# An HGRN and MLA kernel on one core: rotated keys computed a head earlier, work moved between the engines, the last norm by halves

## The chip, the cores and the metric

The kernel runs on one core of a Trainium2 chip. The metric is the device time of one execution in microseconds (us), given as the median of several runs. A core has engines that run side by side, each in the order of its own queue: TensorE (PE in the profile; PEld is its weight load), VectorE (DVE), ScalarE (ACT), GpSimd (POOL), and SyncE (SP), which here only issues DMAs. Matmuls leave their sums in PSUM, and DVE or ACT evacuate them to SBUF.

## The reference, cut to what matters

Two blocks follow one another. The first (SSD mixer with sliding-window attention, then a convolutional FFN) works on 512 tokens and 16 meta tokens. The second, where most of the change lies, is:

```
u  = rms_norm(h)                       # 512 tokens x 1024
hq, hf, hi, hz, cq, ckv, kr, mz, g = split(u @ w_in2)
y1 = hgrn2(hq, hf, hi, hz)             # 8 heads of 128, chunks of 32 tokens
q  = rms_norm(cq)  @ w_uq              # 8 heads of 128 + 64 rotated
k, v = split(rms_norm(ckv) @ w_ukv)    # 8 heads of 128 and 128
k_pe = rope(kr)                        # 64 wide, shared by all heads
y2 = softmax(mask(q_nope k_nope^T + rope(q_pe) k_pe^T)) v * silu(mz)
h  = h + (sigmoid(g1) * (y1 @ wa) + sigmoid(g2) * (y2 @ wb)) @ w_out2
out = rms_norm(h)
```

`rope` takes halves x1, x2 to x1 cos - x2 sin and x2 cos + x1 sin. All is fp32.

## The kernel before, in words

Tokens lie along the free axis and features on the 128 partitions. An fp32 product is made of three products in a faster format (fp32r): activations and weights are each split into a high part and a rest, and `gemm` (L80) issues, per slot of 128 input features, high x high (L88), high weights x rest of the activations (L89) and rest of the weights x high activations (L90). `wload` (L66) brings 512 KB of weights by an SP DMA into one of two `wraw` buffers; ACT copies the high part (`whi`, L76) and DVE subtracts it (`wlo`, L77), or POOL where `eng=nc.gpsimd` is given, as for MLA's `w_uk` and `w_uq` (in `mla_a`, L1111 and L1117). `whi` and `wlo` have three buffers each. PSUM is given out by tags: `g` (2 buffers, for gemms), `a` (3, scores), `t` (2, transposes and sums), `o` (1).

The start (`load`) brings the hidden state, splits it (DVE, `ul`, L62), sums squares on ACT, POOL and DVE, and broadcasts the reciprocal norms R (L129 on PE, L131 on ACT). Projections of the unnormed state start before R is there; R is multiplied in when a result is evacuated (`mulR`, L845).

The second block runs by `Block2.run` (L1203). For each HGRN head h, `hgrn_a(h+1)` projects and prepares the next head and `hgrn_b(h)` runs the chunks; between them stand pieces for MLA (`lora_jobs`): two parts of the latent keys and three of the latent queries with their sums of squares, then at h = 7 their norms and `kpe`. `kpe` (L1043) projects the shared rotated keys, 24 matmuls of 512 columns from a weight tile whose 128 columns hold the 64 features twice, evacuates them times R, rotates them (`rope`, L1077: four DMAs that swap quarters of the partitions, t x sin on DVE L1081, x x cos on POOL L1082, the sum on DVE L1083), and splits them into `kph` (ACT, L1051) and `kpl` (DVE, L1055). `mla_v` (L1085) then makes V, eight groups of six matmuls, each evacuated by ACT with the norm as its scale (`vt`, L1103). For each head, `mla_a` projects keys and queries (and rotates the queries of two heads at a time), `mla_split` splits them (L59 on DVE, `kl` and `ql`), `mla_b` makes scores (L1161 to L1166), the maximum on DVE (L1167), the exponent on ACT, and transposes (L1178), and `mla_c` multiplies by V (L1197).

`output` (L1229) merges the branches with gates. The product with `w_out2` has eight tiles of 128 features: six over all 512 tokens, the last two by halves of 256 tokens. `add` (L1269) adds each to the residual; `SumSq` squares on ACT (L151), adds on POOL (L159) and sums over partitions on PE (L169); `rsqrt` is eleven small DVE steps (L107 to L112). `finish` broadcasts the result over the partitions (PE, L1285), copies it to SBUF (`Rf`, ACT, L1287), multiplies residual, gain and R (six of eight tiles in one DVE step, L1295; the other two on ACT, L1292, and POOL, L1293) and sends each tile of 128 KB out (L1296).

The order on each engine is not that of the code alone: a scheduler places the instructions, moving blocks under `high_priority` forward, and tiles' buffers tie the engines together. In the first block it fills attention's waits on PE with rows of other gemms: `ps_t` L645 are transposes of the probabilities, `pt` L646 and L650 their evacuations on ACT, L655 and L656 the products with the values, `q` L657 the evacuation of a pair of heads, and `gate` L673 a gate between them.

## Time and profile before

| what | value |
|---|---|
| median of three runs | 1815.54 us (1814.12 to 1816.58) |
| profiled execution | 1814.76 us |
| its span, first to last instruction | 1813.0 us |
| mean granted TensorE clock | 0.991 |
| PE busy | 1760.3 us, 12068 matmul records |
| DVE, ACT, POOL busy | 1133.0, 751.5, 319.1 us |

A profile page gives one execution; its views are the busy time of each engine, tables of stretches of time with the clock that TensorE was granted, groups of instructions by line, timelines of an engine, and the chain of waits that ended last. A row such as `1432.79 2.85 DVE lf L1083` says when a step started, how long it took, and where; square brackets at a timeline's row give the idle time before it and what ended it.

### The profile page before, as it was taken

To read this page: it belongs to the slowest core of one execution; us is meant where nothing else is said; L and a number is where in the kernel's file an instruction comes from. 1 tells how busy PE (TensorE), PEld (TensorE's weight loads), DVE (VectorE), ACT (ScalarE), POOL (GpSimd) and SP (SyncE) were. 2 spreads that over 40 slices of the span, in tenths; PEclk is the share of its full clock that TensorE was granted. 3 is DMA by queue.
4 is the path that set the end of the run, shared out by engine and by line. 5 is a ranking of instruction groups with operands and counts; after the bars stand their busy time and mean duration, and the time that the engine had idled before them with its cause. 6 is when DMAs were issued, how large, how long until landed. Compare 5 with 4: busy or idle time off the path is not lost.

```text
span 1813.0 us, 29822 instructions
## 1 busy us (share of the span) xinstructions
PE 1760.3 (97%) x12068; PEld 1588.7 (88%) x12068; DVE 1133.0 (62%) x2140; ACT 751.5 (41%) x1326; POOL 319.1 (18%) x300
## 2 busy tenths in 40 slices
PE   7999999999999999999999999999999999999997
PEld 7989999999989889999999888878888777788886
DVE  7797777855587645466666533576665467743543
ACT  4544444432346643344444433554342445632232
POOL 2154444533320002200000011100000121000112
PEclk9999999999999999999999999999999999999999
DMA  4323232222222122222222222222112121222222
GB/s 146 102 87 104 82 106 83 95 94 94 88 84 76 63 94 94 94 82 94 94 94 94 87 96 96 82 93 70 70 70 93 56 72 48 71 93 93 93 93 71
DMA packets 51311, 158.34 MB, mean 87 GB/s; under 512 B 5923, under 2 KB 9765, under 8 KB 51173
## 3 DMA queue, kind: packets, MB, share of 16 engines
q1 hardware_dynamic: 49252, 153.91, 24.7%
q10 hardware_dynamic: 1872, 2.39, 0.4%
q8 instruction: 95, 1.56, 0.3%
q14 instruction: 44, 0.35, 0.1%
q0 software_dynamic: 48, 0.13, 0.0%
HBM read 152.93 MB, written 2.16 MB: 86 GB/s over the span
## 4 chain that ended last, share of the span: by engine, by line
PE 85%; DVE 7%; ACT 3%; issue 2%; POOL 1%; DMA 1%; SPq 0%; DVEq 0%; POOLq 0%; ACTq 0%
PE ps_g L88 22%; PE ps_g L89 22%; PE ps_g L90 22%; PE ps_g L813 2%; PE ps_g L814 2%; PE ps_g L812 2%; DVE wlo L77 1%; DMA E<-csd 1%; DVE cv L339 1%; PE ps_o L1197 1%; POOL xe L393 1%; PE ps_t L645 1%; PE ps_a L956 1%; PE ps_a L443 1%; PE ps_t L412 1%
## 5 line engine op out<-in xcount | busy, mean ns | idle before, releaser
L76 ACT ACTIVATE whi<-wraw 128x1024 fp32r<-128x1024 f32 (+2 forms) x265 | 274.9, 1038 | 585.9 <-PE ps_g L89 369.8
L77 DVE TENSOR_TENSOR wlo<-wraw,whi 128x1024 fp32r<-128x1024 f32 (+3 forms) x259 | 333.7, 1289 | 152.7 <-ACT whi L76 151.6
L88 PE MATMUL ps_g<-uh,whi 128*128 128x256 f32 (+2 forms) x1056 | 305.5, 289 | 2.4 <-DVE z L186 1.4
L90 PE MATMUL ps_g<-uh,wlo 128*128 128x256 f32 (+2 forms) x1056 | 301.9, 286 | 0.0
L89 PE MATMUL ps_g<-ul,whi 128*128 128x256 f32 (+2 forms) x1056 | 301.2, 285 | 0.0
L88 PEld LDWEIGHTS ps_g<-uh,whi 128*128 128x128 f32 x1056 | 200.2, 190 | 4.8 <-DVE z L186 1.6
L89 PEld LDWEIGHTS ps_g<-ul,whi 128*128 128x128 f32 x1056 | 200.0, 189 | 0.4 <-issue 0.2
L90 PEld LDWEIGHTS ps_g<-uh,wlo 128*128 128x128 f32 x1056 | 199.8, 189 | 0.4 <-issue 0.3
L88 PE MATMUL ps_g<-fh,whi 128*128 128x256 f32 (+1 forms) x704 | 199.1, 283 | 0.8 <-DVE fx L186 0.8
L89 PE MATMUL ps_g<-fl,whi 128*128 128x258 f32 (+1 forms) x704 | 199.5, 284 | 0.0
L90 PE MATMUL ps_g<-fh,wlo 128*128 128x258 f32 (+1 forms) x704 | 198.3, 282 | 0.0
L88 PE MATMUL ps_g<-vh,whi 128*128 128x512 f32 x464 | 185.0, 399 | 1.8 <-DVE lf L845 1.8
L90 PE MATMUL ps_g<-vh,wlo 128*128 128x512 f32 x464 | 184.5, 398 | 0.3 <-DVE wlo L77 0.3
L89 PE MATMUL ps_g<-vl,whi 128*128 128x512 f32 x464 | 184.4, 397 | 0.0
L159 POOL TENSOR_TENSOR sq<-sq 128x514 f32<-128x514 f32 (+2 forms) x48 | 61.9, 1299 | 495.7 <-ACT sq L151 495.7
L88 PEld LDWEIGHTS ps_g<-fh,whi 128*128 128x128 f32 x704 | 133.7, 190 | 1.0 <-DVE fx L186 1.0
L89 PEld LDWEIGHTS ps_g<-fl,whi 128*128 128x128 f32 x704 | 134.0, 190 | 0.0
L90 PEld LDWEIGHTS ps_g<-fh,wlo 128*128 128x128 f32 x704 | 133.6, 190 | 0.0
L88 PEld LDWEIGHTS ps_g<-vh,whi 128*128 128x128 f32 x464 | 87.3, 188 | 20.3 <-ACT whi L76 2.2
L90 PEld LDWEIGHTS ps_g<-vh,wlo 128*128 128x128 f32 x464 | 87.3, 188 | 19.0 <-DVE wlo L77 0.8
L89 PEld LDWEIGHTS ps_g<-vl,whi 128*128 128x128 f32 x464 | 87.4, 188 | 18.9
L88 PE MATMUL ps_g<-yh,whi 128*128 128x256 f32 (+1 forms) x256 | 75.3, 294 | 1.5 <-DVE bt L480 1.1
(434 smaller groups left out, 3834.9 us busy)
## 6 DMA issues: line engine op xcount, KB each, us to landing
wraw<-in_w_in SPq DMA_DIRECT2D x128, 512.0 KB, 3.3
wraw<-in_w_ffn_in SPq DMA_DIRECT2D x44, 512.0 KB, 3.1
E<-csd SPq DMA_DIRECT2D x32, 265.0 KB, 3.9
wraw<-in_w_ssd SPq DMA_DIRECT2D x16, 512.0 KB, 3.2
wraw<-in_w_out SPq DMA_DIRECT2D x16, 512.0 KB, 3.2
wraw<-in_w_ffn_out SPq DMA_DIRECT2D x16, 512.0 KB, 3.2
wraw<-in_w_pab SPq DMA_DIRECT2D x16, 512.0 KB, 3.3
wraw<-in_w_att SPq DMA_DIRECT2D x8, 512.0 KB, 3.3
```

Of the source, the lines that this page charges most:

```text
L76: nc.scalar.activation(hf[:, :n], raw[:, :n], AF.Copy)
L77: (eng or nc.vector).tensor_tensor(lf[:, :n], raw[:, :n], hf[:, :n].bitcast(F32), ALU.subtract)
L88: nc.tensor.matmul(ps, wh, a, start=(i == 0), stop=False)
L89: nc.tensor.matmul(ps, wh, b, start=False, stop=False)
L90: nc.tensor.matmul(ps, wl, a, start=False, stop=(i == last))
L159: self.g.nc.gpsimd.tensor_tensor(a[:, :self.ntok], a[:, :self.ntok], sq[:, :self.ntok], ALU.add)
L339: nc.vector.scalar_tensor_tensor(cv, xr[:, j:j + NT], w(j), cv, ALU.mult, ALU.add)
L393: nc.gpsimd.tensor_tensor(xe[:CH].rearrange("p c (h d) -> p c h d", h=2), xd[:CH, 0:4, :].rearrange("p c (h d) -> p c h d", h=2), dtx(0, 4 ...
L412: nc.tensor.matmul(px[:, c * 128:(c + 1) * 128], bt[:CH, c, :], xe[:CH, c, :], start=True, stop=True)
L812: nc.tensor.matmul(ps, wh, uh, start=(k == 0), stop=False)
L813: nc.tensor.matmul(ps, wh, ul, start=False, stop=False)
L814: nc.tensor.matmul(ps, wl, uh, start=False, stop=(k == NFF - 1))
```

## The change

1. `load`: the broadcast of R is put under high priority.
2. At the start, twelve matmuls of a tile of ones with itself, which nothing uses, are put ahead of the others.
3. `kpe`: the high part and the rest of the 64 weight columns lie side by side in one tile of 128, so that one matmul makes both products with the high activations, and a second one, 64 columns wide, the product with their rest: 16 matmuls instead of 24. Both halves of the partitions are rotated, two further DMAs swap the halves, and DVE adds them. `kpe` is called at h = 6 in place of h = 7.
4. `rope`: x x cos goes from POOL to DVE.
5. `mla_v`: every second group of V is evacuated by DVE.
6. The weights of `mla_a` are split by DVE.
7. `block_input` is called for other heads at a time.
8. `output`: three tiles by halves; the gains are multiplied in on ACT beforehand, so that `finish` has one multiply by R for two tiles of a half (three on DVE, one on POOL) and sends 256 KB at a time.

```diff
-            bcast_rows(g, self.R, rsqrt(g, ps[:88, :6], 88, 6, 1.0 / D, "h"), 88, 6, NT)
+            with g.tc.high_priority():
+                bcast_rows(g, self.R, rsqrt(g, ps[:88, :6], 88, 6, 1.0 / D, "h"), 88, 6, NT)
...
-            self.mulR(k, self.win(base + 2), self.R)
+            with g.tc.high_priority():
+                raw = g.wp.tile([128, 8, 128], F32, name="wraw", tag="wraw", bufs=2)
+                nc.sync.dma_start(out=raw.rearrange("p a b -> p (a b)"), in_=g.a["w_in2"][base + 2])
+                w = g.wp.tile([128, 8, 128], F32R, name="whi", tag="whi", bufs=3)
+                nc.scalar.activation(w[:, :, 0:64], raw[:, :, 0:64], AF.Copy)
+                nc.vector.tensor_tensor(w[:, :, 64:128], raw[:, :, 0:64], w[:, :, 0:64].bitcast(F32), ALU.subtract)
+            ps = psum(g, "g")
+            half = (slice(0, 64), slice(64, 128))
+            for i, (uh, ul) in enumerate(self.u):
...
+                nc.tensor.matmul(ps, w[:, i, :], uh, start=(i == 0), stop=(i == 7))
+                if i == 0:
+                    nc.tensor.matmul(ps[0:64, :], w[:, i, 0:64], ul, start=False, stop=False)
+            self.mulR(k, ps, self.R)
             self.rope(k)
+            t = self.t("th")
+            for r in range(2):
+                nc.sync.dma_start(out=t[half[r], :], in_=k[half[1 - r], :])
+            nc.vector.tensor_tensor(k, k, t, ALU.add)
...
-        nc.gpsimd.tensor_tensor(x, x, self.cosT, ALU.mult)
+        nc.vector.tensor_tensor(x, x, self.cosT, ALU.mult)
...
-                nc.scalar.activation(self.vt[c * 2 + h], ps, AF.Copy, scale=rk[:, c:c + 1])
+                if c % 2:
+                    nc.vector.tensor_scalar(self.vt[c * 2 + h], ps, rk[:, c:c + 1], None, ALU.mult)
+                else:
+                    nc.scalar.activation(self.vt[c * 2 + h], ps, AF.Copy, scale=rk[:, c:c + 1])
...
-            self.wuk = wload(g, g.a["w_uk"][h // 4], eng=nc.gpsimd)
+            self.wuk = wload(g, g.a["w_uk"][h // 4])
...
+            if h == 6:
+                kpe()
             if h == 7:
                 norm("kv")
                 norm("q")
-                kpe()
...
-            for k in ((h,) if h < 6 else (6, 7) if h == 6 else ()):
+            for k in ((h,) if h < 3 else (3, 4) if h == 3 else (5, 6, 7) if h == 4 else ()):
...
-        for ct in range(6):
+        for ct in range(5):
...
+        def gains(i, cts):
+
+            for ct in cts:
+                if ct % 2 == 0:
+                    outs[i, ct // 2] = self.t("y", (128, 2, HN), name="of")
+                nc.scalar.activation(outs[i, ct // 2][:, ct % 2, :], x[ct][:, i * HN:(i + 1) * HN], AF.Copy, scale=pcol(g, "fin2", ct))
...
+            for p in range(4):
+                o = outs[i, p]
+                R = (ps[:, :HN] if p else Rf).unsqueeze(1).broadcast_to([128, 2, HN])
+                (nc.vector if p else nc.gpsimd).tensor_tensor(o, o, R, ALU.mult)
+            for p in (1, 2, 0, 3):
+                (nc.sync, nc.scalar)[p % 2].dma_start(
+                    out=g.a["out"][2 * p:2 * p + 2, :, i * HN:(i + 1) * HN].rearrange("c p t -> p c t"), in_=outs[i, p])
...
+    with tc.high_priority():
+        ps = psum(g, "o")
+        for i in range(12):
+            nc.tensor.matmul(ps[:, :128], g.ones, g.ones, start=(i == 0), stop=(i == 11))
```

Three places show what the scheduler makes of it. First ACT's queue where V is made, before: `vt` is an evacuation of V, `kph` the high part of the rotated keys, `o` and `th` belong to the last HGRN head and the gates, `yhi` to the merge.

```order
L1005 ACTIVATE o<-ps_o,rq_y 128x128 x4
L76 ACTIVATE whi<-wraw 128x1024
L1103 ACTIVATE vt<-ps_g,rq_y 128x512
L1051 ACTIVATE kph<-lf 128x512
L973 ACTIVATE th<-z 128x512
L58 ACTIVATE yhi<-y 128x512
L1103 ACTIVATE vt<-ps_g,rq_y 128x512
L973 ACTIVATE th<-y 128x512
L1103 ACTIVATE vt<-ps_g,rq_y 128x512
```

The same queue in the changed kernel, from `kph` to the third `vt`:

```order
L1072 ACTIVATE kph<-lf 128x512
L974 ACTIVATE th<-z 128x512
...
L131 ACTIVATE lf<-ps_t 128x512
L1127 ACTIVATE vt<-ps_g,rq_y 128x512
L1002 ACTIVATE o,ss<-ps_o 128x128 x4
L131 ACTIVATE lf<-ps_t 128x512
L58 ACTIVATE yhi<-y 128x512
L1127 ACTIVATE vt<-ps_g,rq_y 128x512
L1006 ACTIVATE o<-ps_o,rq_y 128x128 x4
L76 ACTIVATE whi<-wraw 128x1024
L974 ACTIVATE th<-y 128x512
L1127 ACTIVATE vt<-ps_g,rq_y 128x512 x2
```

`kph` has moved out from between the evacuations to before the last head's chunks; the last head's outputs now stand between them, and four of the eight `vt` are on DVE.

Second, DVE's queue at the end before: `h_7` is the last residual tile, `of` an output tile, `rq` the steps of the reciprocal root.

```order
L1269 TENSOR_TENSOR h_7_7934<-ps_g,h_7_7934 128x256
L1295 SCALAR_TENSOR_TENSOR of<-h_0_7927,par,ps_t 128x256
L1295 SCALAR_TENSOR_TENSOR of<-h_1_7928,par,ps_t 128x256
L1295 SCALAR_TENSOR_TENSOR of<-h_2_7929,par,ps_t 128x256
L1295 SCALAR_TENSOR_TENSOR of<-h_4_7931,par,ps_t 128x256
L107 TENSOR_SCALAR rq_m<-ps_t 128x2
L1295 SCALAR_TENSOR_TENSOR of<-h_5_7932,par,ps_t 128x256
L1295 SCALAR_TENSOR_TENSOR of<-h_6_7933,par,ps_t 128x256
L108 TENSOR_SCALAR rq_y<-rq_m 128x2
```

And in the changed kernel, from the same add:

```order
L1295 TENSOR_TENSOR h_7_7947<-ps_g,h_7_7947 128x256
L1324 TENSOR_TENSOR of<-of,ps_t 128x512 x3
L107 TENSOR_SCALAR rq_m<-ps_t 128x2
L108 TENSOR_SCALAR rq_y<-rq_m 128x2
L110 TENSOR_TENSOR rq_u<-rq_y 128x2
...
L112 SCALAR_TENSOR_TENSOR rq_y<-rq_u,rq_y 128x2
L1324 TENSOR_TENSOR of<-of,ps_t 128x512 x3
```

The six multiplies of the first half have become three of twice the width, all ahead of the second half's root, whose steps now follow one another.

Third, PE's queue in the last pair of heads of the first block's attention. `L88` to `L90` are gemm rows that fill a wait. Before:

```order
L645 MATMUL ps_t<-mats,s 128x128 x4
L89 MATMUL ps_g<-ul_106,whi 128x256
...
L655 MATMUL ps_o<-pt,vtok 64x128
L656 MATMUL ps_o<-pt,vtok 64x128
L655 MATMUL ps_o<-pt,vtok 64x128
L656 MATMUL ps_o<-pt,vtok 64x128
```

In the changed kernel:

```order
L646 MATMUL ps_t<-mats,s 128x128 x4
L656 MATMUL ps_o<-pt,vtok 64x128
L657 MATMUL ps_o<-pt,vtok 64x128
L656 MATMUL ps_o<-pt,vtok 64x128
L657 MATMUL ps_o<-pt,vtok 64x128
L646 MATMUL ps_t<-mats,s 128x128 x4
```

In three rounds of that pair, seven, nine and seven gemm rows stood between a transpose and the products that need its evacuation; now none do, and such rows stand in earlier rounds.

## The prediction

> **What bounds the kernel now.** I read the page's head and its shares of the chain first, then a table of equal stretches, then the engines' own rows in the places that the change touches.

> ```profile
> span 1813.0 us, 29822 instructions
> PE 1760.3 (97%) x12068; PEld 1588.7 (88%) x12068; DVE 1133.0 (62%) x2140; ACT 751.5 (41%) x1326; POOL 319.1 (18%) x300
> PE 85%; DVE 7%; ACT 3%; issue 2%; POOL 1%; DMA 1%; SPq 0%; DVEq 0%; POOLq 0%; ACTq 0%
> ```

> TensorE is busy for 97% of the span, and 85% of the chain is its own work. So time can be won in three ways only: fewer matmuls, less PE idle time, and a higher clock. The table by stretches (length; busy us and count of PE, weight loads, DVE, ACT, POOL; granted clock; DMA share; GB/s) says where there is any.

> ```profile
> 861.17:906.50 45.33, 45.33 (x383) 45.33 (x382) 31.29 (x48) 18.75 (x24) 0.00 (x0) 1.00 0.27 94
> 1087.80:1133.12 45.32, 45.32 (x197) 36.70 (x196) 13.65 (x15) 14.48 (x18) 7.69 (x6) 1.00 0.28 96
> 1405.08:1450.40 45.33, 41.01 (x210) 33.66 (x209) 22.22 (x57) 19.89 (x46) 6.45 (x3) 0.96 0.17 56
> 1450.40:1495.72 45.33, 41.17 (x196) 31.89 (x195) 30.33 (x69) 19.62 (x56) 10.77 (x5) 0.96 0.22 72
> 1495.72:1541.05 45.33, 44.52 (x229) 35.49 (x229) 32.64 (x74) 22.73 (x71) 5.80 (x3) 1.00 0.15 48
> 1767.67:1813.00 45.33, 34.45 (x204) 30.30 (x202) 16.81 (x45) 9.81 (x21) 12.48 (x15) 0.91 0.20 71
> ```

> The first two are full: one 512-column matmul costs 45.32/197 = 0.230 us there, one of 256 columns 45.33/383 = 0.118. The passage from HGRN to MLA (A, 1405 to 1450) has 4.3 us without PE, the first MLA heads (B, 1450 to 1496) 4.2, the next stretch 0.8, the end 10.9. These four are what the change can reach beside its matmuls. The clock is below 1.00 in three of them, and finer stretches of 3.41 us show how:

> ```profile
> 1436.20:1439.60 3.40, 1.30 (x6) 1.07 (x7) 2.63 (x4) 2.25 (x5) 0.00 (x0) 1.00 0.06 18
> 1439.60:1443.00 3.40, 3.40 (x10) 2.62 (x9) 0.69 (x1) 1.55 (x3) 0.00 (x0) 0.50 0.00 0
> 1470.34:1473.75 3.41, 1.36 (x4) 0.74 (x5) 3.38 (x4) 3.35 (x13) 1.31 (x1) 1.00 0.32 121
> 1473.75:1477.16 3.41, 3.41 (x9) 2.67 (x8) 1.74 (x6) 0.12 (x2) 0.00 (x0) 0.50 0.23 71
> ```

> A stretch in which PE is busy for only 1.3 to 1.4 us is followed by one at half the clock. At half rate 3.4 us of PE do the work of 1.7, so each costs about 1.6 us beside the idle time itself.

> **The change part by part.** *Matmuls of the rotated keys.* Twenty-four 512-column matmuls become sixteen: 8 x 0.230 = 1.85 us off a full PE. One answer: **-1.85**.

> *Passage A.* The chain of waits there (start, us, what), then POOL's own rows, then DVE's ordinary rows of the same shapes:

> ```profile
> 1432.79 2.85 DVE lf L1083
> 1435.66 0.64 ACT kph L1051
> 1437.67 0.59 ACT vt L1103
> 1438.30 0.50 PE ps_g L1100
> 1469.77 2.43 DVE kl L59
> 1472.85 0.50 PE ps_a L1162
> ```
> ```profile
> 1432.71 2.37 POOL L77 TENSOR_TENSOR wlo<-wraw,whi 128x1024 fp32r<-128x1024 f32 x1
> 1469.29 2.36 POOL L77 TENSOR_TENSOR wlo<-wraw,whi 128x1024 fp32r<-128x1024 f32 x1 [3.33 <-ACT whi L76]
> ```
> ```profile
> 1482.41 0.69 DVE L1081 TENSOR_TENSOR th<-th,kk 128x512 f32<-128x512 f32 x1 [2.13 <-DMA th<-vf]
> 1485.37 1.21 DVE L77 TENSOR_TENSOR wlo<-wraw,whi 128x1024 fp32r<-128x1024 f32 x1
> 1487.31 0.68 DVE L59 TENSOR_TENSOR kl<-ki,kh 128x512 fp32r<-128x512 f32 x1
> ```

> DVE's last step of the rope took 2.85 us where such a step takes 0.69: it began with POOL's weight split (1432.71) and ended 0.56 us after it, so it stood still while POOL ran. `kph` on ACT waited for it, and the first evacuation of V (`vt`) stood behind `kph` in ACT's queue; PE got its buffer back at 1438.30. After the change the rope lies in the seventh head, under gemms; its queue mates there are SP's swap DMAs (two more of 64x512), one DVE add and ACT's `kph`, and behind DVE's wait for the DMAs stands the next gate's evacuation, for which PE has another PSUM buffer. So I cost the moved steps at nothing; without that cover they would be 0.69 on DVE and a DMA round trip, some 3 us. Of the 4.3 us idle I leave 1.3: V's groups of six matmuls take 6 x 0.230 = 1.4 us on nearly one buffer, and an evacuation of 0.6 is then partly seen; DVE taking every second one does not change the first. With the idle time the half-clock stretch at 1439.60 goes, 1.6 more. **-4.6**, between -2.5 (the stretch stays at half rate, 1.8 idle stays) and -6 (no idle).

> [...]

> *Start of MLA, B.* `kl` took 2.43 for 0.68, again over POOL's split (1469.29 to 1471.65), and PE's first scores (1472.85) came behind it. With the six splits on DVE that stall is gone, but DVE does 1.21 more ahead of `kl`: 1.75 - 1.21 = 0.55 earlier. The five cosine products cost DVE 0.69 each; on POOL they were this long:

> ```profile
> L1082 POOL TENSOR_TENSOR vf<-vf,kk 128x512 f32<-128x512 f32 x4 | 7.0, 1753 | 35.7 <-DVE mx L1167 23.0 <-DMA th<-vf 12.7
> ```

> In all DVE takes on 6 x 1.21 + 5 x 0.69 + 4 x 0.6 = 13 us over some 300 us of span and drops near 5 of stalls; it is busy 30 of 45 us here, so it holds. Whether PE reaches enough work in the stretch at 1470 for the clock to stay up I can't read; I take the 0.55 and four tenths of 1.6: **-1.2**, between -4.5 (both half-rate stretch and two more of the gaps gone) and +2 (one more stretch at half rate).

> *The end.* PE's last half product, and DVE's and ACT's rows after it:

> ```profile
> 1799.16 0.28 PE L90 MATMUL ps_g<-nh,wlo 128*128 128x256 f32 x1
> ```
> ```profile
> 1799.48 0.43 DVE L1269 TENSOR_TENSOR h<-ps_g,h 128x256 f32<-128x256 f32 x1 [0.35 <-PE ps_g L90]
> 1800.79 1.66 DVE L1295 SCALAR_TENSOR_TENSOR of<-h,par,ps_t 128x256 f32<-128x256 f32 x4 [0.88 <-ACT Rf L1287]
> 1802.36 0.15 DVE L107 TENSOR_SCALAR rq_m<-ps_t 128x2 f32<-128x2 f32 x1
> 1802.43 0.86 DVE L1295 SCALAR_TENSOR_TENSOR of<-h,par,ps_t 128x256 f32<-128x256 f32 x2
> 1804.96 0.16 DVE L112 SCALAR_TENSOR_TENSOR rq_y<-rq_u,rq_y 128x2 f32<-128x2 f32 x1
> 1806.92 2.44 DVE L1295 SCALAR_TENSOR_TENSOR of<-h,par,ps_t 128x256 f32<-128x256 f32 x6 [1.79 <-ACT Rf L1287]
> ```

> Call the last product's end T = 1799.44. The last mean reached DVE's first step at T+2.92, behind four multiplies of the first half; the eleven steps ended at T+5.68 with two multiplies (0.86) among them; the six multiplies ended at T+9.92. Afterwards the first half's reciprocals are broadcast four matmuls ahead of T, so its three multiplies of 128x512 (0.69 alone, by 1482.41; in a row I estimate 0.6 each, as one of 256 columns is 0.43 alone and 2.44/6 = 0.41 in a row) follow the add, and the mean starts at T+2.4; nothing stands among its steps, so it ends at T+4.5; the same 1.80 to the multiplies, three of 0.6: T+8.2. That is -1.7. The output then leaves in 256 KB pieces:

> ```profile
> bias<-in_bias SPq DMA_DIRECT2D x8, 272.0 KB, 2.7
> out<-of ACTq DMA_DIRECT2D x8, 128.0 KB, 2.1
> ```

> By these a last piece of twice the size lands 0.4 later (0.2 to 1.1). Halving product 5 makes 24 matmuls of 0.230 into 48 of 0.118: +0.15. ACT's early gains lie under PE. **-1.2**, between +0.5 and -2.5.

> *Start.* PE's row, with what it waited for:

> ```profile
> 16.47 0.30 PE L89 MATMUL ps_a<-ul,whi 128*32 128x256 f32 x1 [1.28 <-DVE ul L62]
> 30.99 0.28 PE L283 MATMUL ps_t<-mats,dtf 32*106 32x32 f32 x2 [0.85 <-DVE dtf L279]
> ```

> At 16.47 PE waits for DVE, whatever its clock was before; warm-up matmuls can't move that. The 0.85 before 30.99 waits for R, whose place on PE is the same. **0**, between -0.85 and +1.6 (a half-rate stretch if a warm PE idles more).

> *Order elsewhere.* In the first block's last attention pair the gemm rows that stood between the transposes and the value products are spent earlier.

> ```profile
> 659.47 0.59 PE ps_t L645 x4
> 660.88 0.38 PE ps_o L655 x4
> ```

> Between 660.06 and 660.88 PE ran such rows; without them it sees the evacuation, some 0.7 in each of three rounds, +2.1. ACT reaches the pair's last evacuation without a weight copy and a gate ahead of it, about -1.0. **+1.0** (-1 to +3). The later MLA heads, reordered without a place that I can name, get **+0.5** (-3 to +3, a gap and a half-rate stretch either way).

> **The rivals.** (1) *The start of MLA gets full clock too.* DVE's earlier splits would let the other gaps of B close with the stretch: B becomes -4.5, so 3.3 less. For it: the same stall by POOL stands behind both; against: scores, maxima and evacuations follow one another there anyway. **1804.9**.

> (2) *The gains turn into new waits.* DVE is in order, and in MLA it gets the weight split, the rope and V's evacuations; if these hold up maxima and scores, A gives only -2.5 and B and the later heads +1 each: -1.85 - 2.5 + 1 - 1.2 + 1.0 + 1 = -2.6. For it: DVE is busy 32.6 of 45.3 us in the third MLA stretch already. Against: PE idles only 0.8 there. **1813**.

> (3) *Slower: the first block's attention runs bare.* The order spends gemm rows early; each pair whose three rounds have none left loses 2.1, and 1.6 more if the clock falls, 3.7. One such pair is in the sum. The rest of the sum is -8.35, so it decides from three pairs on (11.1 against 8.35), and four give +6.5: **1822**. For it: the gemm rows form one pool, and the order moves all of them. Against: only the last pair is quite bare, and all the gemm work must still stand somewhere. That the change does not do what it says can hold only for the warm-up, which is costed at nothing.

> **How the numbers follow.** -1.85 - 4.6 - 1.2 - 1.2 + 0 + 1.0 + 0.5 = -7.35. The profiled execution took 1814.76 (span 1813.0 and 1.76 around it): 1807.4. The median of before, 1815.54, stands 0.8 above that execution: **1808.2**. Chances: this sum 0.55 (its own range 1804 to 1811.5), rival 1 0.15, rival 2 0.18, rival 3 0.12. The range 1801.5 to 1814 holds all but rival 3 and the outer ends. A measurement of this kernel can tell 0.2%, 3.6 us, from no change. Faster by more is below 1811.9: the main case, rival 1 and a little of rival 2, 0.74; rival 2 is mostly within it, 0.16; slower 0.10.

> **What would show it.** Right: sixteen key matmuls, no PE gap over 1.5 us between 1405 and 1450 on the old scale and its clock at 1.00, no DVE step of over 2 us beside POOL, last multiply 8.2 us behind the last product. Wrong: a half-rate stretch in A or several in MLA, more PE gaps in the first block's attention than before's one at its end, or a tail as long as it was.

## The result, and the profile after

The changed kernel took 1805.40 us (median of five runs, 1803.93 to 1806.76) against 1815.08 (1814.12 to 1816.58, five runs): a ratio of 0.995, interval 0.9939 to 0.9961, some 9 us faster. The forecast was 1808.2. The profiled execution of the changed kernel was its slowest, 1806.76 with a span of 1805.0, so between the two profiled executions there are only 8.0 us. The head of its page:

```profile
span 1805.0 us, 29863 instructions
PE 1761.6 (98%) x12108; PEld 1590.8 (88%) x12108; DVE 1135.6 (63%) x2151; ACT 753.4 (42%) x1334; POOL 296.2 (16%) x287
PE 85%; DVE 7%; ACT 3%; issue 2%; DMA 1%; POOL 1%; SPq 0%; DVEq 0%; ACTq 0%; POOLq 0%
```

TensorE's busy time is 1.3 us more than before, but the twelve matmuls of ones are in it: up to the first use of R it rises by 4.3, in time that was idle. Behind that, busy time falls by 3.0 and idle time by 4.4. The four stretches of the stage table that had idle time, the first three moved by the 2 us by which the changed kernel arrives there earlier, the last one again the final 45.3 us:

```profile
1403.10:1448.40 45.30, 43.27 (x225) 35.32 (x224) 29.07 (x71) 18.65 (x45) 0.00 (x0) 1.00 0.19 60
1448.40:1493.80 45.40, 43.10 (x210) 32.99 (x208) 30.39 (x72) 18.28 (x57) 0.00 (x0) 0.96 0.20 67
1493.80:1539.10 45.30, 44.11 (x221) 34.75 (x221) 34.78 (x77) 26.04 (x71) 0.00 (x0) 1.00 0.18 57
1759.70:1805.00 45.30, 34.93 (x229) 31.86 (x227) 15.79 (x40) 13.99 (x31) 12.58 (x14) 0.91 0.21 70
```

Passage A lost half of its idle time (4.3 us before, 2.0 now) and runs at full clock; B lost half as well (4.2, now 2.3) but still has one half-rate stretch (0.96). The next stretch and the end hardly changed.

In the chain of waits of the changed kernel, V's evacuations and the start of MLA now read:

```profile
1427.19 0.69 ACT vt L1127
1432.15 0.69 ACT vt L1127
1434.69 0.75 DVE vt L1125
...
1461.69 1.22 DVE wlo L77
1463.04 0.59 DVE kl L59
...
1464.61 0.50 PE ps_a L1186
```

No `kph` and no rope stand among V's evacuations, only the evacuations themselves, 0.7 each. `kl` takes 0.59 where it took 2.43, and a weight split of 1.22 on DVE stands ahead of it. The tail: PE's last product, then DVE.

```profile
1792.21 0.28 PE L90 MATMUL ps_g<-nh,wlo 128*128 128x256 f32 x1
```
```profile
1792.53 0.42 DVE L1295 TENSOR_TENSOR h<-ps_g,h 128x256 f32<-128x256 f32 x1 [2.92 <-PE ps_g L90]
1792.87 1.87 DVE L1324 TENSOR_TENSOR of<-of,ps_t 128x512 f32<-128x512 f32 x3
1794.66 0.15 DVE L107 TENSOR_SCALAR rq_m<-ps_t 128x2 f32<-128x2 f32 x1
...
1796.62 0.16 DVE L112 SCALAR_TENSOR_TENSOR rq_y<-rq_u,rq_y 128x2 f32<-128x2 f32 x1
1798.57 1.89 DVE L1324 TENSOR_TENSOR of<-of,ps_t 128x512 f32<-128x512 f32 x3 [1.79 <-ACT Rf L1320]
```

With T = 1792.49 the mean starts at T+2.17, the root ends at T+4.29 and the multiplies at T+7.97, where the forecast had 2.4, 4.5 and 8.2. The span ends at T+12.47 against T+13.55 before.

Cut at PE's starts behind the same gaps, the two executions differ in this way: to the first use of R -0.7; on to the end of the SSD groups -0.4; first attention up to the FFN -0.9; FFN 0; HGRN, V and the start of MLA (1192.05 to 1504.03 before, 1190.08 to 1495.30 after) -6.8; from there to the last product +1.8; tail -1.1. Together -8.0. In the stretch of -6.8 PE's busy time falls from 302.7 to 300.1 and its idle time from 9.3 to 5.1.

### The profile page after: what moved, and what is told of

Read it like the earlier page. It is cut to its first block, busy times and chain, and to the rows that moved or that the text cites. A ratio compares the mean times of both kernels' runs of the same rounds, so it can differ in the third digit from the quotient of the medians.

```text
span 1805.0 us, 29863 instructions
## 1 busy us (share of the span) xinstructions
PE 1761.6 (98%) x12108; PEld 1590.8 (88%) x12108; DVE 1135.6 (63%) x2151; ACT 753.4 (42%) x1334; POOL 296.2 (16%) x287
## 4 chain that ended last, share of the span: by engine, by line
PE 85%; DVE 7%; ACT 3%; issue 2%; DMA 1%; POOL 1%; SPq 0%; DVEq 0%; ACTq 0%; POOLq 0%
PE ps_g L88 22%; PE ps_g L89 21%; PE ps_g L90 21%; PE ps_g L814 2%; PE ps_g L815 2%; PE ps_g L813 2%; DVE wlo L77 1%; DVE cv L340 1%; DMA E<-csd 1%; PE ps_o L1221 1%; POOL xe L394 1%; PE ps_t L646 1%; PE ps_a L957 1%; PE ps_t L413 1%; PE ps_a L444 1%
## 5 line engine op out<-in xcount | busy, mean ns | idle before, releaser
L76 ACT ACTIVATE whi<-wraw 128x1024 fp32r<-128x1024 f32 (+3 forms) x264 | 273.8, 1038 | 555.3 <-PE ps_g L89 336.6
L77 DVE TENSOR_TENSOR wlo<-wraw,whi 128x1024 fp32r<-128x1024 f32 (+3 forms) x264 | 339.9, 1288 | 142.6 <-ACT whi L76 141.8
L88 PE MATMUL ps_g<-uh,whi 128*128 128x256 f32 (+2 forms) x1056 | 303.8, 288 | 2.4 <-DVE z L186 1.4
L90 PE MATMUL ps_g<-uh,wlo 128*128 128x256 f32 (+2 forms) x1056 | 301.8, 286 | 0.0
L89 PE MATMUL ps_g<-ul,whi 128*128 128x256 f32 (+2 forms) x1056 | 301.1, 285 | 0.0
L88 PEld LDWEIGHTS ps_g<-uh,whi 128*128 128x128 f32 x1056 | 199.4, 189 | 4.5 <-DVE z L186 1.6
L88 PE MATMUL ps_g<-fh,whi 128*128 128x256 f32 (+1 forms) x704 | 199.1, 283 | 0.8 <-DVE fx L186 0.8
L89 PEld LDWEIGHTS ps_g<-ul,whi 128*128 128x128 f32 x1056 | 199.4, 189 | 0.5 <-issue 0.2
L90 PEld LDWEIGHTS ps_g<-uh,wlo 128*128 128x128 f32 x1056 | 199.4, 189 | 0.4 <-issue 0.3
L89 PE MATMUL ps_g<-fl,whi 128*128 128x258 f32 (+1 forms) x704 | 199.6, 284 | 0.0
L90 PE MATMUL ps_g<-fh,wlo 128*128 128x258 f32 (+1 forms) x704 | 198.5, 282 | 0.0
L88 PE MATMUL ps_g<-vh,whi 128*128 128x512 f32 x456 | 181.8, 399 | 2.3 <-DVE lf L846 1.8
L89 PE MATMUL ps_g<-vl,whi 128*128 128x512 f32 x456 | 181.8, 399 | 0.0
L90 PE MATMUL ps_g<-vh,wlo 128*128 128x512 f32 x456 | 181.4, 398 | 0.3 <-DVE wlo L77 0.3
L88 PEld LDWEIGHTS ps_g<-fh,whi 128*128 128x128 f32 x704 | 133.8, 190 | 1.0 <-DVE fx L186 1.0
L89 PEld LDWEIGHTS ps_g<-fl,whi 128*128 128x128 f32 x704 | 134.1, 190 | 0.0
L90 PEld LDWEIGHTS ps_g<-fh,wlo 128*128 128x128 f32 x704 | 133.6, 190 | 0.0
L88 PEld LDWEIGHTS ps_g<-vh,whi 128*128 128x128 f32 x456 | 85.8, 188 | 20.9 <-ACT whi L76 2.2
L89 PEld LDWEIGHTS ps_g<-vl,whi 128*128 128x128 f32 x456 | 85.9, 188 | 18.5
L90 PEld LDWEIGHTS ps_g<-vh,wlo 128*128 128x128 f32 x456 | 85.8, 188 | 18.5 <-DVE wlo L77 0.8
L88 PE MATMUL ps_g<-yh,whi 128*128 128x256 f32 (+1 forms) x256 | 75.3, 294 | 1.5 <-DVE bt L481 1.1
```

The source lines that it names most:

```text
L76: nc.scalar.activation(hf[:, :n], raw[:, :n], AF.Copy)
L77: (eng or nc.vector).tensor_tensor(lf[:, :n], raw[:, :n], hf[:, :n].bitcast(F32), ALU.subtract)
L88: nc.tensor.matmul(ps, wh, a, start=(i == 0), stop=False)
L89: nc.tensor.matmul(ps, wh, b, start=False, stop=False)
L90: nc.tensor.matmul(ps, wl, a, start=False, stop=(i == last))
```

## The experiments

My theory is the forecast's: ACT's queue and DVE's standstill behind POOL made passage A's gap (3.32 us in the trace of before), the half clock read behind it (0.50 from 1439.60) goes with it, and the tail gains by its order. The rivals are that only one of the two made the gap, that the clock has another cause, and that DVE's added work is paid for elsewhere. One execution of the kernel before differs from another by up to 8 us (1810.3 to 1818.4 over all runs below), so the intervals are about 2 us wide either way. The traces give places and causes, but each of them is one execution.

**Start alone, with and without the priority of R.** The kernel before with

```diff
+    with tc.high_priority():
+        ps = psum(g, "o")
+        for i in range(12):
+            nc.tensor.matmul(ps[:, :128], g.ones, g.ones, start=(i == 0), stop=(i == 11))
```

and, in the first of the two, R's broadcast under high priority.

> The kernel before with the change's start alone: the broadcast of R under high priority and the twelve matmuls of ones. The order of the first block's attention stays that of before. My theory: PE's wait for DVE before 16.47 us is not moved by a warm clock, so 0 against before (-0.7 to +0.5). Rival: the clock is what counts, all matmuls up to 12.65 us at full rate, -1.7 to -2.

> The kernel before with the twelve matmuls of ones alone, without the priority of R. The scheduler then also gives the first block's attention the order that the changed kernel has (no gemm rows in the last pair's three rounds). The forecast's term for that order: +1.0, so +1.0 against the run with the start alone. Rival, from the changed kernel's trace: the half-rate stretch behind the last pair goes because the gap there is shorter, and pays for the rounds, -1 against the run with the start alone.

Both: 0.9985, interval 0.9976 to 0.9994, against the kernel before (1812.19 and 1812.55, before 1815.23), so -2.7 +- 1.6. In both traces the attention has the changed kernel's order; what I wrote for the first, that it keeps the order of before, did not hold, so the two do not tell start and order apart by their difference. The 0 expected of the start missed as well, and the rival's -1.7 to -2 lies in the interval; the traces show how much of that is the start. PE's start behind the gap at R stands at 30.3 to 30.7 us in the nine profiled executions with the ones, and at 30.7 to 31.0 in those without: some 0.4. From the end of the SSD groups to the FFN, the rows of the kernel before and of the changed one:

```profile
501.99 1.11 PE L129 MATMUL ps_o<-mats,rq_y 103*128 103x103 f32 x8 [1.93 <-DVE rq_y L112]
774.10 0.58 PE L88 MATMUL ps_g<-fh,whi 128*128 128x258 f32 x1 [0.84 <-DVE fx L186]
```
```profile
500.91 1.11 PE L129 MATMUL ps_o<-mats,rq_y 103*128 103x103 f32 x8 [1.94 <-DVE rq_y L112]
772.11 0.39 PE L88 MATMUL ps_g<-fh,whi 128*128 128x258 f32 x1 [0.84 <-DVE fx L186]
```

272.1 against 271.2, and 271.2 in both runs here: the order that the forecast charged with 1.0 gains 0.9 in this pair. Why, the rows at the last pair of heads show, of the kernel before and of the changed one:

```profile
667.41 0.62 PE L88 MATMUL ps_g<-ah,whi 128*128 128x256 f32 x3 [2.05 <-ACT ah L58]
```
```profile
665.05 0.45 PE L656 MATMUL ps_o<-pt,vtok 128*64 128x128 f32 x4 [0.15 <-ACT pt L647]
666.94 0.61 PE L88 MATMUL ps_g<-ah,whi 128*128 128x256 f32 x3 [1.23 <-ACT ah L58]
```

The bare rounds cost PE 0.15 in all, ahead of the last one, and not 0.7 each, since the transposes of the next round run while a round is evacuated; and the gap behind the pair falls from 2.05 to 1.23. With it goes the half-rate stretch that followed at 668: all six profiled executions with the order of before have one there, none of the seven with the changed order.

**Rotated keys alone.** The kernel before with the side-by-side product and its place at h = 6, nothing else (edit as in the change's diff).

> The kernel before with the rotated keys' product in 16 matmuls and called a head earlier, and nothing else: splits and cosine products stay on POOL, all V evacuations on ACT. If ACT's queue (kph between the evacuations of V) made the gap of 3.3 us and the half-rate stretch behind it, both go with the move: -1.85 and about -3 to -4, together -5 to -6. Rival: DVE standing still behind POOL made it, and as POOL keeps its work the stall comes back at another place: -1.85 to -2.5.

0.9966 (0.9953 to 0.9978), 1808.49 against 1815.23: -6.2 (-4.0 to -8.5). In the trace, from 1192.20 to 1499.62, it takes 4.6 us less than before there; no half-rate stretch in A, and the largest wait for a `vt` is 0.78 where it was 3.32 (PE's row before, then PE's rows here):

```profile
1438.30 0.50 PE L1100 MATMUL ps_g<-whi,lf 128*128 128x512 f32 x1 [3.32 <-ACT vt L1103]
```
```profile
1430.81 1.13 PE L129 MATMUL ps_t<-mats,rq_y 128*128 128x128 f32 x8 [1.17 <-DVE rq_y L112]
1434.12 0.50 PE L1120 MATMUL ps_g<-whi,lf 128*128 128x512 f32 x1 [0.78 <-ACT vt L1123]
```

POOL still stops DVE, as its row and DVE's show:

```profile
1427.63 2.41 POOL L77 TENSOR_TENSOR wlo<-wraw,whi 128x1024 fp32r<-128x1024 f32 x1 [22.75 <-DVE rq_u L110]
```
```profile
1428.11 2.48 DVE L974 SCALAR_TENSOR_TENSOR z<-th,z 128x512 f32<-128x512 f32 x1 [0.32 <-ACT th L973]
```

The same step takes 0.68 at 1410.61 in this trace, with no POOL step beside it; here it takes 2.48 and ends 0.55 behind POOL's. It costs PE 1.17, not 3.3, since V's evacuations no longer wait for it. So the move out of ACT's queue is by itself enough for the gap at V and the half-rate stretch behind it, and the rival's -1.85 to -2.5 is out; PE's waits in A fall from 4.3 to 3.0, not to the 2.0 of the changed kernel.

**Engines alone.** The kernel before with MLA's splits and the cosine products on DVE, and every second V evacuation there:

```diff
-            self.wuk = wload(g, g.a["w_uk"][h // 4], eng=nc.gpsimd)
+            self.wuk = wload(g, g.a["w_uk"][h // 4])
-        nc.gpsimd.tensor_tensor(x, x, self.cosT, ALU.mult)
+        nc.vector.tensor_tensor(x, x, self.cosT, ALU.mult)
+                if c % 2:
+                    nc.vector.tensor_scalar(self.vt[c * 2 + h], ps, rk[:, c:c + 1], None, ALU.mult)
```

> The kernel before with the engines' work moved alone: MLA's weight splits and the cosine products on DVE, every second V evacuation on DVE; the rotated keys stay where they were. My theory: the step of 2.85 us takes 0.7 and the gap of 3.3 us shrinks by some 2, the half-rate stretch of passage A then goes or not, and B gains 0.5 to 1.2: -2.5 to -5. Rival: DVE's added work gives it back as waits in MLA's heads: 0 to +2.

0.9978 (0.997 to 0.9987), 1811.22: -4.0 (-2.4 to -5.4). The rope still stands among V's evacuations, but runs at its own pace, and PE's wait is short (DVE's row, then PE's):

```profile
1430.82 0.69 DVE L1083 TENSOR_TENSOR lf<-lf,th 128x512 f32<-128x512 f32 x1
```
```profile
1434.56 0.51 PE L1100 MATMUL ps_g<-whi,lf 128*128 128x512 f32 x1 [0.99 <-DVE vt L1104]
```

PE's waits in A add up to 2.0, as in the changed kernel, and the half-rate stretch is gone: of the fourteen profiled executions here, the four with the long gap have one behind it, the other ten none. So either cure alone takes most of A's loss away, this one all that the change took: the long gap needed both, the step that POOL stretched and the queue that carried it on to V. The parts' gains can't be added: -6.2 and -4.0 alone, with the start (-2.7) some 13, and some 9 together.

**Changed kernel without the ones.** The twelve matmuls taken out.

> The changed kernel without the twelve matmuls of ones; the scheduler then orders the first block's attention as before the change. By the traces so far the start is worth 0.3 and the attention's order 0.5 to 0.9: about 1 us slower than the changed kernel. Rival: what the two runs with the start showed by their medians, 2.7 slower. The forecast's +1.0 for the order would make it 1 us faster.

0.9973 (0.9962 to 0.9984), 1809.82 against 1814.61, 3.7 to 4.4 slower than the changed kernel's two medians (1805.40, and 1806.17 below); its profiled execution is 1.9 longer. The attention stretch takes 274.5 (271.2 with the ones), with three more half-rate stretches in or right behind it. By the medians order and start are worth some 3 to 4 us (2.7 in the two runs above), where the forecast had the order alone cost 1.0; the interval overlaps that of the second median. The traces account for less. PE's order in the attention is here, row for row, that of the kernel before, and with that order the stretch took 272.1 before, 274.4 with the keys alone, 271.7 with the engines alone and 271.8 with the output alone. The 274.4 and the 274.5 have two half-rate stretches more than the other three, a second one behind 500 and one at 528. With the changed order it took 271.2 in six executions, and 274.2 in the run with the late gaps filled, again with two more. So the order gains 0.5 to 0.9 and the start 0.4; whether the order also makes the other half-rate stretches rarer, or they fell by chance, is not shown. That twelve unused matmuls change the order 500 us later is shown: the one run differs from the changed kernel, the other from the kernel before, by nothing else.

**Changed kernel with MLA's splits on POOL again.**

```diff
-            self.wuk = wload(g, g.a["w_uk"][h // 4])
+            self.wuk = wload(g, g.a["w_uk"][h // 4], eng=nc.gpsimd)
```

and the same for `w_uq`.

> The changed kernel with MLA's weight splits on POOL again (six of 128x1024). If ACT's queue alone made passage A's gap, A stays as after the change, and only the start of MLA loses the 0.5 to 1.2 that the stall of kl costs: +0.5 to +1.5 against the changed kernel. Rival: the stall behind POOL rules in A too: +3 to +4, with DVE steps of over 2 us there.

0.9968 (0.9956 to 0.998), 1808.94: some 3 slower by the medians, with intervals that overlap, where 0.5 to 1.5 were expected and the rival had 3 to 4. Its sign, a DVE step of over 2 us in A, is there (2.51 at 1425.48, beside POOL's split), but PE waits only 1.20 behind it. In all PE's gaps grow by 2.0, 0.7 in A (no half rate) and 1.3 from B on, where the stall is back:

```profile
1462.49 2.36 POOL L77 TENSOR_TENSOR wlo<-wraw,whi 128x1024 fp32r<-128x1024 f32 x1 [3.33 <-ACT whi L76]
```
```profile
1462.97 2.43 DVE L59 TENSOR_TENSOR kl<-ki,kh 128x512 fp32r<-128x512 f32 x1 [0.44 <-ACT kh L58]
```

The profiled execution, without a half-rate stretch in B, is even 0.9 shorter than the changed kernel's, so the size stays open. One thing the trace settles: from the gap at the end of MLA's start to the last product it needs 296.1, the changed kernel 297.2. The splits cost 1.1 there when they stand on DVE.

**Output alone**, and the **output in 128 KB pieces**. The second is the changed kernel with

```diff
+                for c in range(2):
+                    (nc.sync, nc.scalar)[c].dma_start(out=g.a["out"][2 * p + c, :, i * HN:(i + 1) * HN], in_=outs[i, p][:, c, :])
```

> The kernel before with the change's output alone (three tiles by halves, gains ahead on ACT, multiplies by R in pairs, 256 KB pieces). The forecast's term is -1.2; the changed kernel's trace, from the last product's end to the span's end, gives 13.56 - 12.47 = 1.1 less, and the halved tile costs 0.15 to 0.4 of it: -0.7 to -1.1. Rival: the early gains on ACT and the added halves disturb the products ahead: 0 to +1.

> The changed kernel with its output sent in 128 KB pieces, both tiles of a pair on two queues, as many DMAs as before the change. If the larger pieces are what takes 0.9 us of the tail back, the stretch from the last multiply's end to the span's end falls from 4.5 to 3.6 us. Rival: it is the number of DMAs behind each other on a queue that ends last: no change or longer.

Output alone: 0.9997 (0.9988 to 1.0006), not told apart from none. In its trace the span ends 12.4 behind the last product (13.55 before), 1.15 less, but from the gap at the end of MLA's start to the last product it needs 296.1 where before needs 295.4: the halved tile costs 0.7, so 0.5 is left. The pieces of 128 KB: 0.9957 (0.9944 to 0.997), and from the last multiply's end to the span's end 4.4 us, as against 4.5 with 256 KB and 3.6 before. By the views of transfers, the middle time to landing on the two queues is 2.9 and 3.3 us for 256 KB, 2.1 and 2.5 for 128 KB here. What counts is the last piece, by the traces' issue and landing times. Before the change it is issued 0.07 behind the last multiply's end and lands 2.43 later; in the changed kernel 0.09 and 3.26; with the pieces of 128 KB 0.46 and 2.79, since each queue issues twice as many, at some 0.4 each, and the last waits its turn. From there to the span's end it is 1.1 to 1.2 in all three. So the larger piece is what takes back 0.8 of the 0.9, and the smaller ones lose by their number what they gain by their size.

**Gaps filled.** Three kernels with matmuls that nobody uses, meant for places where PE waits. The first has 23; the second only the nine of late places, with PE's order otherwise the changed kernel's; the third the nine and ten of 512 columns ahead of the second and fourth SSD group's broadcast. The form, in `bcast_rows`, and in `mla_b` for the second head:

```diff
+        for _ in range(warm if c0 == 0 else 0):
+            if wt is None:
+                nc.tensor.matmul(ps[:, :rows], g.ms[:rows, 0:1].broadcast_to([rows, 128]), g.ident[:rows, :rows], start=True, stop=True)
+            else:
+                nc.tensor.matmul(ps, wt[:, :128], wt[:, :512], start=True, stop=True)
...
+            for _ in range(4 if (h, b) == (1, 3) else 0):
+                nc.tensor.matmul(ps[:, :n], kn2[0][:, :128], kn2[0][:, :n], start=True, stop=True)
```

> The changed kernel with 23 matmuls more, whose results nothing uses, at the places where PE waits: five behind the first step of a reciprocal root in the second and fourth SSD group and ahead of the FFN, four ahead of the third pair's state product, four ahead of the second MLA head's scores. The waits are as long as before, but PE is busy in part of them. If a stretch with under some 1.9 us of PE work in it is what halves the clock for the next 3.4, the half-rate stretches at 127, 267, 503, 773 and 1465 us go, about 1.6 each: -5 to -8 against the changed kernel. [...]

> The changed kernel with nine matmuls more, whose results nothing uses: five behind the first step of the reciprocal root ahead of the FFN (gaps of 0.91 and 0.84 at 769 to 772 us) and four ahead of the second MLA head's scores (1.17 and 0.38 at 1462 to 1464). PE's order is otherwise the changed kernel's, unlike in the run with all gaps filled. If too little PE work in a stretch halves the clock, both half-rate stretches go, 1.6 each: -2 to -3.2 against the changed kernel run beside it. Rival: the added work only moves the waits, 0 to +1.5.

> The run with the late gaps filled and, in the second and fourth SSD group, five matmuls of 512 columns over the whole array ahead of the reciprocal root's broadcast, in place of the narrow ones that left the clock at half behind 269 and 501 us. The scheduler gives the first block's attention the order of before. If it is the work in the array that the clock follows and not the time for which PE is busy, the half-rate stretches at 270 and 503 go as well: -2 to -4 beyond the late gaps alone, less about 2 for the attention's order. Rival: still half behind both.

> The changed kernel once more, beside the two runs with filled gaps: 8 to 10 us under the kernel before, with five to seven half-rate stretches.

Against the kernel before: 0.9972 (0.9959 to 0.9985) with all gaps filled narrowly, where the scheduler moved the attention to a third order; 0.995 (0.9937 to 0.9962) with the late ones, 0.9948 (0.9937 to 0.996) with all and wide ones, 0.9957 (0.9944 to 0.997) for the changed kernel beside them. The last three can't be told apart by time; 1804.85 is the lowest median of this study, no more. So by time the first two missed what was expected: 5 to 8 below the changed kernel (1808.61 is 2.4 and 3.2 above its two medians) and 2 to 3.2 below it (1805.50 is 0.7 below the 1806.17 beside it). The third, 1804.85, fits its 2 to 4 less some 2 for the order, but within the noise. The stretches of 3.41 us tell more. First the changed kernel, run again, at the FFN's start and the second MLA head, then the run with the late gaps filled, at the same places of its program:

```profile
766.66:770.07 3.41, 1.73 (x14) 1.38 (x12) 1.40 (x8) 0.66 (x2) 0.00 (x0) 1.00 0.44 154
770.07:773.48 3.41, 3.33 (x15) 3.33 (x16) 2.19 (x5) 0.81 (x1) 0.00 (x0) 0.51 0.00 0
1459.57:1462.98 3.41, 1.82 (x10) 0.91 (x8) 3.41 (x8) 3.35 (x10) 0.00 (x0) 1.00 0.33 103
1462.98:1466.40 3.42, 3.42 (x10) 2.56 (x9) 2.19 (x7) 1.58 (x8) 0.00 (x0) 0.51 0.20 70
```
```profile
772.00:775.41 3.41, 2.57 (x23) 2.40 (x22) 1.48 (x8) 0.66 (x2) 0.00 (x0) 1.00 0.45 154
775.41:778.83 3.42, 3.42 (x30) 3.42 (x30) 2.35 (x5) 1.32 (x2) 0.00 (x0) 1.00 0.02 5
1464.90:1468.31 3.41, 2.71 (x12) 1.47 (x10) 3.38 (x8) 3.35 (x10) 0.00 (x0) 1.00 0.37 123
1468.31:1471.72 3.41, 3.41 (x17) 2.74 (x17) 2.94 (x8) 1.73 (x8) 0.00 (x0) 1.00 0.18 58
```

PE still waits there for others (2.57 and 2.71 busy), but the clock stays at 1.00 behind it. This is no accident of one execution: the half-rate stretch at the FFN's start stands in all eleven without the fill and in none of the three with it, the one at the second MLA head in all four executions of the changed kernel that have neither the fill nor the splits on POOL, and in none of the three. From the FFN's gap to where PE stops at 1188.8 the filled kernel takes 413.6 us, the unfilled one, from 770.15 to 1185.26, 415.1: one half-rate stretch is worth 1.5, close to the 1.6 of the sum. That this execution was not shorter for it (1808.36, the slowest of its six) goes with the other gaps: it had seven half-rate stretches elsewhere (31, two at 127, 502, 513, 526 and 1192 us), the unfilled one four (268, 500, 770 and 1463), where five to seven were expected.

At the second SSD group's broadcast, where the first kernel has five narrow matmuls and the third five wide ones, the same two stretches of each:

```profile
268.88:272.30 3.42, 2.18 (x24) 1.77 (x23) 2.97 (x7) 0.66 (x2) 1.15 (x2) 0.99 0.53 140
272.30:275.71 3.41, 3.41 (x19) 2.81 (x18) 1.54 (x5) 0.28 (x1) 0.24 (x1) 0.50 0.05 19
```
```profile
268.49:271.90 3.41, 2.17 (x24) 1.86 (x24) 2.51 (x7) 0.52 (x1) 1.15 (x2) 1.00 0.52 155
271.90:275.32 3.42, 3.42 (x30) 2.87 (x28) 2.17 (x8) 0.58 (x3) 1.72 (x2) 1.00 0.22 68
```

PE was busy equally long, 2.18 and 2.17 us; the clock fell in one and not in the other. It is tempting to put this down to the fills, but PE's rows of the fills and of the broadcast show that neither fill stands in its stretch (first kernel, then third):

```profile
261.25 1.26 PE L129 MATMUL ps_o<-mats,rq_m 103*128 103x103 f32 x10
268.42 1.14 PE L132 MATMUL ps_o<-mats,rq_y 103*128 103x103 f32 x8
```
```profile
260.20 1.33 PE L132 MATMUL ps_o<-yh 128*128 128x512 f32 x5
267.38 1.14 PE L135 MATMUL ps_o<-mats,rq_y 103*128 103x103 f32 x8
```

The scheduler put both some 6 us ahead of the broadcast, with other work between. So this pair does not test what the wide fills were put in for; the two stretches only cut the same part of the program at different points. This third kernel's profiled execution had three half-rate stretches (128, 664 and 1187 us), the fewest of all here, and the shortest span, 1801.9; that the wide fills did it is not shown.

## Why the prediction was right, point by point

- **Matmuls of the keys, -1.85**: right; the sixteen take 3.7 us at 0.231 each.
- **Passage A, -4.6**: right in mechanism, a little large. Gaps 4.3 to 2.0 and one half-rate stretch of 1.6 make -3.9; 2.0 us of waits stayed where I left 1.3, among them those for ACT's evacuations (0.33 and 0.78) and one for DVE's (0.48). The prediction had the two causes one behind the other; that curing either one takes most of it, the runs of the parts alone showed.
- **Start of MLA, -1.2**: right in its cause, by another split. The gaps shrank by 1.9 (4.9 to 3.0), not 0.55, since `kl` came 1.8 faster and others with it; the half-rate stretch, of which I took four tenths, stayed (PE 1.84 us busy ahead of it in the profiled execution, 1.82 in the repeat). With keys and A this would make -7.7 from HGRN to MLA's start, where -6.8 was measured: gaps give 4.1 of it, the matmuls and the half-rate stretch together 2.6 of busy time, not 3.5. Where the other 0.9 went I can't say.
- **Tail, -1.2**: the order of its steps was right to 0.25 us. The halved tile was mis-sized, 0.7 for 0.15, and so was the output's end, 0.9 for 0.4, since the last piece of 256 KB landed 0.83 later than one of 128 KB did: about -0.4 in all.
- **Start, 0**: -0.4; DVE's `ul` still ends the wait that was at 16.47.
- **Attention's order, +1.0**: this step failed, in sign. "Some 0.7 in each of three rounds" was read from a filled gap's length; the bare rounds cost 0.15 in all, and the shorter gap behind the pair spared a half-rate stretch: -0.5 to -0.9 by the traces with the same number of half-rate stretches otherwise. The 3 to 4 that the medians give the order and the start together are not accounted for.
- **Later MLA heads, +0.5**: +1.1. From MLA's start to the last product the engines alone need 296.5 where the kernel before and the keys alone need 295.4; with the halved tile that makes the changed kernel's 297.2. DVE's added work is paid for there, as rival 2 said, but with 1.1 and not with the whole gain. It is the weight splits: with them on POOL again the stretch takes 296.1, just the 0.7 of the halved tile more than before.

The sum was -7.35 and the profiled pair shows -8.0. That they lie so close is in part luck: the failed step (1.9 too high) and the stretches up to the SSD groups' end, costed at nothing and measured at -1.1, went against the terms that promised too much (keys, A and B by 0.9, the tail with its halved tile by 0.8, the heads by 0.6). Rival 3's mechanism, bare rounds, is in the order but does not cost what it was priced at.

## What to carry to other kernels

Before costing a gap, ask how many causes hold it open: here a stretched step and an in-order queue made it together, and curing either took most of it, so gains of parts alone don't add. Before reading an inserted fill's effect, look where the scheduler put it. A fill that stands in a wait is not the wait's length: look whether the waiting engine's input would be ready anyway. And an edit that looks local (twelve unused matmuls at the start) can reorder work 500 us away when a scheduler places it: compare the order on the engine that bounds the kernel, everywhere.

## What the runs showed of the hardware that I had not expected

The clock does not follow the profile's busy time alone. At 2.17 and 2.18 us it stayed or fell, and in the run with the keys alone it fell behind a stretch in which PE was busy throughout; four of the fourteen executions show this, at 521 to 524 us:

```profile
524.30:527.71 3.41, 3.41 (x29) 3.26 (x29) 3.15 (x12) 1.36 (x6) 1.18 (x1) 1.00 0.43 139
527.71:531.13 3.42, 3.42 (x18) 3.42 (x17) 2.25 (x16) 3.42 (x13) 0.59 (x2) 0.50 0.18 48
```

Of the 29 matmuls in it, 16 are only two columns wide, and they make 1.9 us of its busy time:

```profile
L580 PE MATMUL ps_t<-pth,vm 32*128 32x2 f32 x16 | 1.9, 247 | 0.0
```

What else it follows is not shown.

A gap at the same place of the program is followed by half rate in one execution and not in the next: the one of 2.95 us at 122.96 was in the changed kernel's first profiled execution (PE busy for 1.48 us of the window) and not in its repeat, which I put down to the phase of the steps. The fourteen profiled executions had three to eight half-rate stretches. One costs up to 1.7 us by my estimate (3.41 us at a clock of 0.50) and can cost nothing: the attention took 271.2 us with one behind 500 us and with two, since a wait at 510 us got shorter (1.33 us in the run with the splits on POOL, 0.18 in the one with 128 KB pieces). That half-rate stretches make part of the spread between runs of one kernel is borne out by the clocks on record: of the 68 runs of the kernel before that stand beside the experiments, the 10 with a mean granted clock of 0.992 took 1811.3 us on average, the 17 with 0.989 took 1816.2.
